# Strassen operands formed inside the evacuation of the first feed-forward block, an earlier input load, and a projection partly in single PSUM banks

## The chip, the cores and the metric

The kernel runs on one NeuronCore of a Trainium2 chip. Its five engines work from their own in-order queues and meet through semaphores: TensorE (PE in the profile, PEld for its weight loads), VectorE (DVE), ScalarE (ACT), GpSimd (POOL) and SyncE (SP), which issues every DMA here. The metric is the device time of one execution in microseconds, the median of several runs.

## The reference

One decoder layer runs on 512 prompt tokens and 8 single-token sequences, 520 columns in all, with a model width of 1024. Two recurrent branches come first. The part that matters here follows them:

```python
hm = rms_norm(r, norm_mlp_g)
r = r + jnp.square(jax.nn.relu(hm @ w_ff1)) @ w_ff2          # 1024 -> 4096 -> 1024
hp = rms_norm(r, norm_ple_g)
r = r + jax.nn.sigmoid(hp @ w_ple_gate) * (p_l @ w_ple_proj)  # per-layer inputs p_l, 256 wide
```

All of it is float32 work. A final RMS norm gives the outputs.

## The kernel before, in words

**Products in three passes.** Activations lie with channels on the 128 partitions and the 520 columns along the free side, cut in two halves of 260. Every operand is split into a rounded high part and a low rest (`H` and `L` for activations, `wh` and `wl` for weights), and each product is the sum of wh·H, wh·L and wl·H. A *unit* is one block of 128 output channels: 8 blocks of the contraction times 3 passes times 2 halves, so 48 matmuls of 128x128x260 into one PSUM tile `m`, which takes two banks. The pool of `m` has two buffers, so the third unit from now needs the tile of this one emptied. A second pool, `s`, has four single banks.

**The order.** There is no scheduler: `flow` is a list that the code writes by hand, and all engines get their instructions in that order. `run_unit(u)` first calls `prep_all()`, which prepares the weights of the item two places later in the list: ACT rounds `raw` to `wh` (L208), DVE subtracts to get `wl` (L213), and SP issues the next weight load. Then come the first 24 matmuls, the functions hooked to this unit in `at[u]`, the other 24 matmuls, and the unit's evacuation `evac`.

**The feed-forward part.** It computes 4096 hidden channels. The first quarter (1024) uses 8 plain units, `ff1`. Their evacuation `ev_ff1(i)` does relu times the norm's factor on DVE (tile `hid`, L942), the square on ACT (L943), and the split: the high part on ACT (L581), the low part on DVE (L582), into `fa` or `fb`. The other three quarters use a Strassen-Winograd scheme with seven products instead of eight: 12 *pairs* n = 0 to 11, each in four steps `(n, 0)` to `(n, 3)` of 24, 24, 24 and 12 matmuls into single banks X, Z and Y. Four sums of activations per contraction block kp = 0 to 3 are needed ahead of pair 0. `combine_a(kp)` scales two blocks of the residual stream (`hn`, L979, two instructions) and splits them into `comb`; `combine_b(kp)` forms four sums (`hs`, L994 to L997) and splits them into `comb` too. Before the change these are hooks in `at`, one to each ff1 unit from the second on, the last on the first unit of the following ff2 quarter.

**The second matrix.** `ff2` units turn a finished quarter of hidden channels back into the residual stream `xT` (L949). They are laid between the steps of the pairs: `(n,0)`, unit, `(n,1)`, `(n,2)`, unit, `(n,3)`. Two of the first quarter's ff2 units stand ahead of pair 0. That leaves six, so pairs 2 and 3 have no unit between `(n,0)` and `(n,1)`. A step's bank is read by ACT or DVE before a later product is added on top of it (L1037 is the copy of X that the product of `(n,1)` waits for).

**The projection.** `p_load` loads the per-layer inputs `pn` (SP, L1061) from a hook on the first ff2 unit of the last quarter, into the space S0 of a `comb` tile. `p_split` transposes them on PE (L1071) from a hook on the second. Two projection units follow. Each holds four groups of 12 matmuls, every group in an `m` tile, evacuated by one ACT copy per group (`pj`, L1084).

Of the kernel before, what the change touches and what calls it, by code (L numbers as in the profile page):

```python
# [45 lines left out]
def decoder_step_kernel(  # L46
# [179 lines left out]
    def mm(w, k, xh, xl, ps, first, last):  # L226
        wh, wl = w
        for i, (a, b) in enumerate(((wh, xh), (wh, xl), (wl, xh))):
            for z in range(2):
                PE.matmul(ps[:, z, :NH], lhsT=a[:, k, :], rhs=b[:, z * NH:(z + 1) * NH],  # L230
                          start=first and i == 0, stop=last and i == 2)

    psum_of = {}
# [1 line left out]
    def run_groups(u, lo, hi):  # L235

        due = []
        n = 0
        for gi, (slots, start, stop, evac) in enumerate(units[u].groups):
            for si, (k, xs) in enumerate(slots):  # L240
                if lo <= n < hi:
                    if si == 0 and start:
                        psum_of["cur"] = pm.tile([128, 2, 512], F32, tag="m", name="m")
                    ps = psum_of["cur"]
                    xh, xl = xs()
                    mm(w_of[u], k, xh, xl, ps, start and si == 0, stop and si == len(slots) - 1)
                    if si == len(slots) - 1 and evac is not None:
                        due.append((evac, ps))
                n += 1
        return due  # L250

    def run_unit(u):
        prep_all()
        if u in extra:
            prep_all()
        due = run_groups(u, 0, 4)
        for f in at.pop(u, []):
            f()
        for e, ps in due:
            e(ps[:, :, :NH])  # L260
        for e, ps in run_groups(u, 4, 8):
            e(ps[:, :, :NH])
        w_of.pop(u)

    def unit(w, c, H, L, evac):
# [670 lines left out]
    def ev_ff1(i):  # L936
        def ev(ps):
            if i == 0:
                mx["hid"] = pair("X2", "hid")
                hid_slots(0)  # L940
            t = mx["hid"][:, i % 2]
            V.scalar_tensor_tensor(h2(t), in0=ps, scalar=0.0, in1=h2(mx["rstd"]), op0=ALU.max, op1=ALU.mult)  # L942
            S.activation(t, t, AF.Square)  # L943
            split(hid[0][0][i], hid[0][1][i], t)
        return ev

    def ev_ff2(q, j):
# [21 lines left out]
    z0, z1 = slice(0, NH), slice(NH, N)  # L969

    def combine_a(kp):
        def go():
            r4 = lambda t: big.tile([128, 4, NH], F32R, tag=t, name="comb")
            if kp == 0:
                comb["A22"] = r4("S8"), r4("S9")
            n = comb["n"] = pair("S7", "hn")
            for h in range(2):
                j = kp + 4 * h
                V.scalar_tensor_tensor(n[:, h], in0=xT[:, j], scalar=cv[:, V_MLP + j:V_MLP + j + 1], in1=mx["rstd"],  # L979
                                       op0=ALU.mult, op1=ALU.mult)  # L980
            t = r4(f"S{10 + kp}")
            comb["A1", kp] = t[:, 0:2], t[:, 2:4]
            comb["S", kp] = r4(f"S{14 + kp}" if kp < 2 else f"S{kp - 2}"), r4(("S2", "S4", "S5", "S6")[kp])
            split(*comb["A1", kp], n[:, :, z0])
            H, L = comb["A22"]
            split(H[:, kp], L[:, kp], n[:, 1, z1])
        return go

    def combine_b(kp):
        def go():  # L990
            n = comb["n"]
            a11, a12, a21, a22 = n[:, 0, z0], n[:, 1, z0], n[:, 0, z1], n[:, 1, z1]
            t = big.tile([128, 4, NH], F32, tag="X0", name="hs")
            V.tensor_tensor(t[:, 0], a21, a22, op=ALU.subtract)  # L994
            V.tensor_tensor(t[:, 2], a11, a21, op=ALU.subtract)
            V.tensor_tensor(t[:, 1], t[:, 0], a11, op=ALU.subtract)
            V.tensor_tensor(t[:, 3], t[:, 1], a12, op=ALU.add)  # L997
            split(*comb["S", kp], t)
        return go
# [19 lines left out]
    def finish(q, slot, t):  # L1019
        S.activation(t, t, AF.Square)  # L1020
        split(hid[q][0][slot], hid[q][1][slot], t)

    def run_pair(n, i):

        q = 1 + n // 4
        slot = 2 * (n % 4)
        t1, t2 = mx["hid"][:, 0], mx["hid"][:, 1]
        prep_all()
        if i == 0:
            if slot == 0:  # L1030
                hid_slots(q)
# [3 lines left out]
        if i == 0:  # L1035
            product(n, 0, 0, "A11", X, True)
            S.activation(r1, X, AF.Copy)  # L1037
            product(n, 0, 1, "S1", Z, True)
            S.activation(r5, Z, AF.Copy)
        elif i == 1:  # L1040
            product(n, 1, 0, "S2", X, False)
            S.activation(r2, X, AF.Copy)
            Y = bank()[:, 0:NH]
            product(n, 1, 1, "A12", Y, True)
            V.tensor_tensor(t1[:, z0], r1, Y, op=ALU.add)
        elif i == 2:
            product(n, 2, 0, "S3", X, False)
            V.tensor_tensor(t2[:, z1], r5, X, op=ALU.subtract)
            product(n, 2, 1, "S4", Z, False)
            V.tensor_tensor(t2[:, z0], Z, r2, op=ALU.subtract)  # L1050
            S.activation(t2, t2, AF.Relu)
            finish(q, slot + 1, t2)
        else:
            S.activation(t1[:, z0], t1[:, z0], AF.Relu)
            product(n, 3, 0, "A22", X, False)
            S.activation(t1[:, z1], X, AF.Relu)
            finish(q, slot, t1)

    def p_load():
        mx["pn"] = big.tile([128, 4, 256], F32, tag="S0", name="pn")  # L1060
        dma(mx["pn"], p_prompt[0, 0].rearrange("(c p) d -> p c d", p=128))  # L1061
        dma(vd, p_sample[0, :, 0])

# [15 lines left out]
    def ev_proj(j):  # L1079
        def ev(ps):  # L1080
            if j == 0:
                for a in range(4):
                    mx["pj", a] = pair(f"S{8 + a}", "pj")
            S.activation(h2(mx["pj", j // 2][:, j % 2]), ps, AF.Copy, scale=0.5)  # L1084
# [9 lines left out]
        pair_src[n] = w1[:, :, 1024 + n * 256:1280 + n * 256]  # L1094
    flow = list(range(len(units)))
    ff2 = ff2_quarter(0)
    flow += ff2[:2]
    for kp in range(4):
        at[u_ff + 1 + 2 * kp].append(combine_a(kp))
        at[u_ff + 2 + 2 * kp].append(combine_b(kp))  # L1100
    ff2 = ff2[2:]
    for q in range(1, 4):
        per = (2, 2, 1, 1) if q == 1 else (2, 2, 2, 2)
        for n, m in zip(range(4 * q - 4, 4 * q), per):
            x, y = ff2[:m - 1], ff2[m - 1:m]
            ff2 = ff2[m:]
            flow += [(n, 0), *x, (n, 1), (n, 2), *y, (n, 3)]
        ff2 = ff2_quarter(q)
    u_proj = len(units)
# [8 lines left out]
                dma(rv[:, k], wpj[:, k, i * 512:(i + 1) * 512].rearrange("p (o n) -> p o n", n=128))  # L1118
        units.append(Unit(ld, groups))
    flow += [ff2[0], ff2[1], u_proj, u_proj + 1, *ff2[2:]]  # L1120
    at[ff2[0]].append(p_load)
    at[ff2[1]].append(p_split)


# [122 lines left out]
    plan_loads()  # L1247

    def run_ple():
        mx["gt"] = pair("S7", "gt").rearrange("p a n -> p (a n)")  # L1250
        mx["y"] = big.tile([128, 4, D], F32, tag="B1", name="y")
        mx["yd"] = big.tile([8, D], F32, tag="S6", name="yd")
        steps = defaultdict(list)
        for a, when in enumerate(((5, 7, 8, 10), (13, 14))):
            for jp, i in enumerate(when):
# [298 lines left out]
```

## Time and profile before

| | |
|---|---|
| median of three timed runs | 1118.9 us (1118.26 to 1120.29) |
| profiled execution, its own time | 1120.74 us |
| its span, first to last instruction | 1118.8 us |
| mean granted TensorE clock | 0.994 |
| PE busy | 1095.2 us (98%) |
| DVE busy | 652.6 us (58%) |
| ACT busy | 478.4 us (43%) |
| DMA moved | 123.01 MB, 110 GB/s mean |

Times in the views are microseconds from the first instruction, unless marked ns. A timeline row gives start, duration, engine, line, operation, output<-inputs, shapes, the number of merged instructions, and in brackets the idle time of that engine before it with what ended it. Busy PE time is an overlapped sum, so what a wait costs is read from the starts of PE's instructions. The waits view lists the total, the number and the longest of each kind of wait. The window view gives the busy time and number of instructions of each engine in a stretch, then the granted PE clock and the DMA's share and rate.

### The profile page before, as it was taken

Reading aid. Unit: us, or ns where it says so; the run is one execution under the profiler, and the core shown is the slowest. Engines: PE = TensorE matmul, PEld = TensorE weight load, DVE = VectorE, ACT = ScalarE, POOL = GpSimd, SP = SyncE. Lnnn points to the kernel's source line nnn. Section 1 sums busy time; section 2 is a strip of 40 time slices with the busy share of each in tenths; the row PEclk is TensorE's granted clock in tenths of the full one; section 3 lists DMA queues with packets and bytes.
Section 4 is the critical chain, followed back from the end, with each engine's and each line's share of the span. In section 5 each row is a group of like instructions: output and inputs, shape, how many; then the busy total and the mean of one; then the engine's idle time right before and its main releaser. Section 6 shows DMA issues by size and latency. Waiting matters only on the chain.

```text
span 1118.8 us, 23371 instructions
## 1 busy us (share of the span) xinstructions
PE 1095.2 (98%) x10289; PEld 1075.1 (96%) x10289; DVE 652.6 (58%) x989; ACT 478.4 (43%) x765; POOL 24.4 (2%) x19
## 2 busy tenths in 40 slices
PE   8999999999999999999999999799899999999997
PEld 8999999999999999999999999799899999999997
DVE  6576767859656754442342555665756666653665
ACT  6322534343344425422222244434545445544465
POOL 1000000000011011000000000000000000000001
PEclk9999999999999999999999999989999999999999
DMA  6535252533445365433333232223232432343401
GB/s 218 152 96 170 82 170 73 157 105 115 136 138 156 114 173 154 118 95 95 95 88 101 77 95 76 76 76 95 76 114 77 114 112 76 103 133 87 112 20 77
DMA packets 218740, 123.01 MB, mean 110 GB/s; under 512 B 3960, under 2 KB 217216, under 8 KB 218512
## 3 DMA queue, kind: packets, MB, share of 16 engines
q1 hardware_dynamic: 218640, 121.54, 37.7%
q8 instruction: 80, 1.31, 0.5%
q14 instruction: 20, 0.16, 0.0%
HBM read 109.89 MB, written 11.63 MB: 109 GB/s over the span
## 4 chain that ended last, share of the span: by engine, by line
PE 93%; DVE 3%; ACT 3%; DMA 1%; issue 1%; SPq 0%; DVEq 0%; ACTq 0%
PE m L230 67%; PE s L1014 10%; PE m L1279 2%; PE s L1279 2%; PE s L363 1%; PE s L482 1%; ACT wh L208 1%; DVE wl L213 1%; PE s L765 1%; PE s L519 1%; PE s L543 1%; PE s L722 1%; DVE comb L582 1%; DMA pn<-in_p_prompt_dram 0%; PE s L545 0%
## 5 line engine op out<-in xcount | busy, mean ns | idle before, releaser
L213 DVE TENSOR_TENSOR wl<-raw,wh 128x1024 fp32r<-128x1024 f32 (+1 forms) x141 | 172.8, 1227 | 128.5 <-ACT wh L208 128.0
L230 PE MATMUL m<-hH,wh 128*128 128x260 f32 x1120 | 230.9, 287 | 0.0
L230 PE MATMUL m<-hH,wl 128*128 128x260 f32 x1120 | 226.0, 283 | 0.0
L230 PE MATMUL m<-hL,wh 128*128 128x260 f32 x1120 | 225.2, 283 | 0.0
L208 ACT ACTIVATE wh<-raw 128x1024 fp32r<-128x1024 f32 (+1 forms) x141 | 147.3, 1046 | 84.8 <-PE m L230 78.9
L230 PEld LDWEIGHTS m<-hH,wh 128*128 128x128 f32 x1120 | 172.3, 188 | 3.4 <-issue 1.7
L230 PEld LDWEIGHTS m<-hH,wl 128*128 128x128 f32 x1120 | 172.5, 188 | 0.0
L230 PEld LDWEIGHTS m<-hL,wh 128*128 128x128 f32 x1120 | 172.5, 188 | 0.0
L1014 PE MATMUL s<-comb,wh 128*128 128x260 f32 x672 | 122.4, 283 | 3.1 <-ACT cst L1037 3.1
L1014 PEld LDWEIGHTS s<-comb,wh 128*128 128x128 f32 x672 | 103.8, 188 | 3.5 <-ACT cst L1037 3.5
L1014 PE MATMUL s<-comb,wl 128*128 128x260 f32 x336 | 95.1, 283 | 0.0
L230 PE MATMUL m<-fa,wh 128*128 128x260 f32 x384 | 69.3, 291 | 3.7 <-DVE hid L942 2.0
L1014 PEld LDWEIGHTS s<-comb,wl 128*128 128x128 f32 x336 | 63.2, 188 | 0.0
L230 PEld LDWEIGHTS m<-fa,wh 128*128 128x128 f32 x384 | 57.1, 196 | 4.1 <-issue 2.2
L230 PE MATMUL m<-fa,wl 128*128 128x260 f32 x256 | 52.6, 288 | 0.0
L230 PE MATMUL m<-fl,wh 128*128 128x260 f32 x256 | 52.2, 286 | 0.0
L230 PE MATMUL m<-fh,wh 128*128 128x260 f32 x256 | 52.1, 285 | 0.0
L230 PE MATMUL m<-fh,wl 128*128 128x260 f32 x256 | 51.9, 284 | 0.0
L949 DVE TENSOR_TENSOR xT<-xT,m 128x520 f32<-128x520 f32 x32 | 22.3, 696 | 40.7 <-PE m L230 40.7
L164 ACT ACTIVATE wh<-cst 128x512 fp32r<-128x512 f32 x36 | 22.8, 633 | 43.5 <-DVE cst L170 29.1
L230 PEld LDWEIGHTS m<-fa,wl 128*128 128x128 f32 x256 | 40.6, 194 | 0.0
L230 PEld LDWEIGHTS m<-fh,wl 128*128 128x128 f32 x256 | 40.1, 192 | 0.0
(356 smaller groups left out, 2000.5 us busy)
## 6 DMA issues: line engine op xcount, KB each, us to landing
raw<-in_w_in_dram SPq DMA_DIRECT2D x72, 512.0 KB, 3.9
raw<-in_w_ff_dram SPq DMA_DIRECT2D x40, 512.0 KB, 4.1
rawp<-in_w_ff_dram SPq DMA_DIRECT2D x24, 512.0 KB, 3.7
vbc<-vdd SPq DMA_DIRECT2D x16, 512.0 KB, 4.2
Sd<-in_state_hgrn_dram SPq DMA_DIRECT2D x8, 512.0 KB, 8.0
out_dram<-Sd SPq DMA_DIRECT2D x8, 512.0 KB, 5.4
rSd<-in_state_ret_dram SPq DMA_DIRECT2D x8, 512.0 KB, 5.9
out_dram<-rSd SPq DMA_DIRECT2D x8, 512.0 KB, 3.5
```

What stands on the lines that cost most here:

```text
L164: S.activation(wh[:, 4 * h:4 * h + 4], x, AF.Copy)
L208: S.activation(wh[:, k], r[:, k], AF.Copy)
L213: e1.tensor_sub(wl[:, k], r[:, k], wh[:, k])
L230: PE.matmul(ps[:, z, :NH], lhsT=a[:, k, :], rhs=b[:, z * NH:(z + 1) * NH], start=first and i == 0, stop=last and i == 2)
L363: PE.matmul(b[32 * j:32 * j + 32, 32 * hc:32 * hc + 32], lhsT=kx[:, h, o:o + 32], rhs=qx[:, h, o:o + 32], start=True, stop=True)
L482: PE.matmul(b[32 * i:32 * i + 32, :], lhsT=q[g], rhs=Sd[g][:, 4 * z:4 * z + 4, :], start=True, stop=True)
L519: PE.matmul(b[:, c * 128:(c + 1) * 128], lhsT=kn[:, h, c, :], rhs=vn[:, h, c, :], start=True, stop=True)
L543: PE.matmul(o, lhsT=vn[:, h, c, :], rhs=A[:, h * 4 + c, :], start=True, stop=c == 0)
L582: V.tensor_sub(L, x, H)
L949: V.tensor_tensor(h2(xT[:, j]), h2(xT[:, j]), ps, op=ALU.add)
L1014: PE.matmul(out, lhsT=w[:, 4 * half + k, :], rhs=x, start=start and k == 0 and m == 0, stop=k == 3 and m == 2, skip_group_check=not start)
L1279: PE.matmul(ps, lhsT=w[:, k, :], rhs=x, start=k == 0 and n == 0, stop=k == 7 and n == 2)
```

## The change

1. **Sums inside the evacuation.** `combine_a` and `combine_b` no longer are hooks. `ev_ff1(i)` calls one of them itself: a for even i, b for odd i. It puts the DVE arithmetic between the square and the split, appends ACT's high parts of `comb` behind the split, and leaves only DVE's subtractions as a hook of the next unit.
2. **Order of the first quarter's pairs.** One ff2 unit instead of two stands ahead of pair 0. Pairs 0, 1 and 2 have two units each. Pair 3 has the one between `(3,0)` and `(3,1)` and none between `(3,2)` and `(3,3)`. In `(3,2)` the weight preparation moves from the step's start to behind the first product's DVE subtraction (`prep_last`).
3. **Load of the per-layer inputs.** `p_load` is hooked one unit earlier, to the last ff2 unit of the third quarter, and its tile lies in S7 (the old `hn`). `gt` moves from S7 to S6, and `yd` from S6 to S7.
4. **Projection banks.** In each projection unit groups 0 and 1 keep an `m` tile. Groups 2 and 3 take two single banks each and are evacuated by two ACT copies of 260 columns.

The diff, cut to its core:

```diff
@@ run_groups @@
-                        psum_of["cur"] = pm.tile([128, 2, 512], F32, tag="m", name="m")
-                    ps = psum_of["cur"]
+                        if gi < 2:
+                            t = pm.tile([128, 2, 512], F32, tag="m", name="m")
+                            psum_of["cur"] = t[:, :, :NH], [t[:, z, :NH] for z in range(2)]
+                        else:
+                            psum_of["cur"] = None, [bank()[:, :NH] for z in range(2)]
+                    both, ps = psum_of["cur"]
...
@@ ev_ff1 @@
             S.activation(t, t, AF.Square)
+            cuts = combine_b(i // 2) if i % 2 else combine_a(i // 2)
             split(hid[0][0][i], hid[0][1][i], t)
+            for c in cuts:
+                S.activation(c[0], c[2], AF.Copy)
+            at[u_ff + i + 1].append(lambda: [V.tensor_sub(x, y, h) for h, x, y in cuts])
...
@@ run_pair @@
-        prep_all()
+        if (n, i) not in prep_last:
+            prep_all()
...
             product(n, 2, 0, "S3", X, False)
             V.tensor_tensor(t2[:, z1], r5, X, op=ALU.subtract)
+            if (n, i) in prep_last:
+                prep_all()
             product(n, 2, 1, "S4", Z, False)
...
@@ p_load @@
-        mx["pn"] = big.tile([128, 4, 256], F32, tag="S0", name="pn")
+        mx["pn"] = big.tile([128, 4, 256], F32, tag="S7", name="pn")
...
@@ ev_proj @@
+            out = mx["pj", j // 2][:, j % 2]
+            if isinstance(ps, list):
+                for z in range(2):
+                    S.activation(out[:, z * NH:(z + 1) * NH], ps[z], AF.Copy, scale=0.5)
+            else:
+                S.activation(h2(out), ps, AF.Copy, scale=0.5)
...
@@ flow @@
-    flow += ff2[:2]
-    for kp in range(4):
-        at[u_ff + 1 + 2 * kp].append(combine_a(kp))
-        at[u_ff + 2 + 2 * kp].append(combine_b(kp))
-    ff2 = ff2[2:]
+    flow += ff2[:1]
+    ff2 = ff2[1:]
     for q in range(1, 4):
-        per = (2, 2, 1, 1) if q == 1 else (2, 2, 2, 2)
+        per = (2, 2, 2, 1) if q == 1 else (2, 2, 2, 2)
...
-            x, y = ff2[:m - 1], ff2[m - 1:m]
+            x, y = ff2[:1], ff2[1:m]
             ff2 = ff2[m:]
+            if not y:
+                prep_last.add((n, 2))
             flow += [(n, 0), *x, (n, 1), (n, 2), *y, (n, 3)]
...
-    at[ff2[0]].append(p_load)
+    at[ff2[0] - 1].append(p_load)
```

**Where instructions move.** The first place is DVE's queue in the ff1 units, from one `hid` to the next. Before:

```order
L942 SCALAR_TENSOR_TENSOR hid<-m,x_7811 128x520
L582 TENSOR_TENSOR fb<-hid,fa 128x520
L213 TENSOR_TENSOR wl<-raw,wh 128x1024
L994 TENSOR_TENSOR hs<-hn 128x260
L995 TENSOR_TENSOR hs<-hn 128x260
L996 TENSOR_TENSOR hs<-hs,hn 128x260
L997 TENSOR_TENSOR hs<-hs,hn 128x260
L582 TENSOR_TENSOR comb<-hs,comb 128x1040
L942 SCALAR_TENSOR_TENSOR hid<-m,x_7811 128x520
```

And in the changed kernel, on the same stretch (fb is the low part of the split, wl that of the weights two units ahead):

```order
L947 SCALAR_TENSOR_TENSOR hid<-m,x_7811 128x520
L999 TENSOR_TENSOR hs<-hn 128x260
L1000 TENSOR_TENSOR hs<-hn 128x260
L1001 TENSOR_TENSOR hs<-hs,hn 128x260
L1002 TENSOR_TENSOR hs<-hs,hn 128x260
L587 TENSOR_TENSOR fb<-hid,fa 128x520
L214 TENSOR_TENSOR wl<-raw,wh 128x1024
L953 TENSOR_TENSOR comb<-hs,comb 128x1040
L947 SCALAR_TENSOR_TENSOR hid<-m,x_7811 128x520
```

The four sums stand right behind `hid` instead of behind `wl`. The subtraction stays last. ACT's rounding of `comb` moves in the same way, from behind `wh` to ahead of it.

The second place is ACT's queue from the last step of pair 2 on, in the changed kernel: steps `(3,1)`, `(3,2)`, `(3,3)` and the beginning of what follows. L1048 is the copy in `(3,1)`. L1059 to L586 are the relu, square and high part of the pair's second block. L1062 and L1064 are the two relus in `(3,3)`, of which L1064 empties bank X:

```order
L165 ACTIVATE wh<-cst 128x512
L1048 ACTIVATE cst<-s 128x260
L165 ACTIVATE wh<-rawp 128x512
L165 ACTIVATE wh<-cst 128x512
L1059 ACTIVATE hid<-hid 128x520
L1024 ACTIVATE hid<-hid 128x520
L586 ACTIVATE fh<-hid 128x520
L209 ACTIVATE wh<-raw 128x1024
L1062 ACTIVATE hid<-hid 128x260
L1064 ACTIVATE hid<-s 128x260
```

Before, the same pair's ACT rows, from its copy in `(3,1)`, were these:

```order
L1042 ACTIVATE cst<-s 128x260
L164 ACTIVATE wh<-cst 128x512
L1051 ACTIVATE hid<-hid 128x520
L1020 ACTIVATE hid<-hid 128x520
L581 ACTIVATE fh<-hid 128x520
L164 ACTIVATE wh<-rawp 128x512
L164 ACTIVATE wh<-cst 128x512
L208 ACTIVATE wh<-raw 128x1024
L1054 ACTIVATE hid<-hid 128x260
L1056 ACTIVATE hid<-s 128x260
```

The two half roundings (rawp and cst) move from behind the split to ahead of the relu. The unit that stood ahead of `(3,3)` is gone, so all of this falls into fewer matmuls.

The third place is SP's queue of loads, before:

```order
L965 DMA raw<-in_w_ff_dram 128x8x128 x3
L1118 DMA raw<-in_w_ple_proj_dram 128x4x128 x4
L965 DMA raw<-in_w_ff_dram 128x8x128 x2
L1061 DMA pn<-in_p_prompt_dram 128x4x256
L1062 DMA vd<-in_p_sample_dram 8x256
L224 DMA raw<-in_w_ple_gate_dram 128x8x128
```

And now:

```order
L974 DMA raw<-in_w_ff_dram 128x8x128 x3
L1130 DMA raw<-in_w_ple_proj_dram 128x4x128 x4
L1069 DMA pn<-in_p_prompt_dram 128x4x256
L1070 DMA vd<-in_p_sample_dram 8x256
L974 DMA raw<-in_w_ff_dram 128x8x128 x2
L225 DMA raw<-in_w_ple_gate_dram 128x8x128
```

The inputs `pn` and `vd` pass two weight loads.

More of the change, by code (lines that the diff above doesn't have):

```diff
@@ L118, in decoder_step_kernel @@
     extra = set()
+    prep_last = set()
     raw_of, w_of = {}, {}
@@ L229, in mm @@
             for z in range(2):
-                PE.matmul(ps[:, z, :NH], lhsT=a[:, k, :], rhs=b[:, z * NH:(z + 1) * NH],
+                PE.matmul(ps[z], lhsT=a[:, k, :], rhs=b[:, z * NH:(z + 1) * NH],
                           start=first and i == 0, stop=last and i == 2)
@@ L247, in run_groups @@
                     if si == len(slots) - 1 and evac is not None:
-                        due.append((evac, ps))
+                        due.append((evac, both if both is not None else ps))
                 n += 1
@@ L259, in run_unit @@
         for e, ps in due:
-            e(ps[:, :, :NH])
+            e(ps)
         for e, ps in run_groups(u, 4, 8):
-            e(ps[:, :, :NH])
+            e(ps)
         w_of.pop(u)
@@ L971, in combine_a @@
     def combine_a(kp):
[L972 to L986, printed above, removed]
@@ L987, in combine_a @@
-        return go
-    def combine_b(kp):
[L990 to L999, printed above, removed]
+        r4 = lambda t: big.tile([128, 4, NH], F32R, tag=t, name="comb")
@@ new lines, in combine_a @@
+        if kp == 0:
+            comb["A22"] = r4("S8"), r4("S9")
+        n = comb["n"] = pair("S7", "hn")
+        for h in range(2):
+            j = kp + 4 * h
+            V.scalar_tensor_tensor(n[:, h], in0=xT[:, j], scalar=cv[:, V_MLP + j:V_MLP + j + 1], in1=mx["rstd"],
+                                   op0=ALU.mult, op1=ALU.mult)
+        t = r4(f"S{10 + kp}")
+        comb["A1", kp] = t[:, 0:2], t[:, 2:4]
+        comb["S", kp] = r4(f"S{14 + kp}" if kp < 2 else f"S{kp - 2}"), r4(("S2", "S4", "S5", "S6")[kp])
@@ new lines, in combine_a @@
+        return (*comb["A1", kp], n[:, :, z0]), (*(x[:, kp] for x in comb["A22"]), n[:, 1, z1])
+    def combine_b(kp):
+        n = comb["n"]
+        a11, a12, a21, a22 = n[:, 0, z0], n[:, 1, z0], n[:, 0, z1], n[:, 1, z1]
+        t = big.tile([128, 4, NH], F32, tag="X0", name="hs")
+        V.tensor_tensor(t[:, 0], a21, a22, op=ALU.subtract)
+        V.tensor_tensor(t[:, 2], a11, a21, op=ALU.subtract)
+        V.tensor_tensor(t[:, 1], t[:, 0], a11, op=ALU.subtract)
+        V.tensor_tensor(t[:, 3], t[:, 1], a12, op=ALU.add)
+        return (*comb["S", kp], t),
@@ L1083, in ev @@
                     mx["pj", a] = pair(f"S{8 + a}", "pj")
-            S.activation(h2(mx["pj", j // 2][:, j % 2]), ps, AF.Copy, scale=0.5)
+            out = mx["pj", j // 2][:, j % 2]
[4 more added lines that the diff above has]
+                S.activation(h2(out), ps, AF.Copy, scale=0.5)
         return ev
@@ L1249, in run_ple @@
     def run_ple():
-        mx["gt"] = pair("S7", "gt").rearrange("p a n -> p (a n)")
+        mx["gt"] = pair("S6", "gt").rearrange("p a n -> p (a n)")
         mx["y"] = big.tile([128, 4, D], F32, tag="B1", name="y")
-        mx["yd"] = big.tile([8, D], F32, tag="S6", name="yd")
+        mx["yd"] = big.tile([8, D], F32, tag="S7", name="yd")
         steps = defaultdict(list)
```

## The prediction

> **What bounds the kernel now.** I read the chain of waits first, then PE's waits, then PE's own starts where the waits are.
>
> ```profile
> PE 93%; DVE 3%; ACT 3%; DMA 1%; issue 1%; SPq 0%; DVEq 0%; ACTq 0%
> 468.38 206.89 PE m L230 x1728
> ```
>
> The chain is PE nearly throughout. Its undisturbed stretch gives the pitch: 206.89 / 1728 = 0.1197 us a matmul, so 5.75 us a unit of 48 and 1.44 us a product of 12. The change keeps every matmul, so it can win only what PE waits.
>
> ```profile
> PE m L230 <- DVE hid L942: 5.8, 4, 2.0
> PE m L1371 <- DMA xs<-in_x_sample_dram: 3.4, 1, 3.4
> PE s L1014 <- ACT cst L1037: 3.1, 2, 1.6
> PE m L230 <- ACT fa L581: 1.7, 1, 1.7
> PE s L1071 <- DMA pn<-in_p_prompt_dram: 1.3, 1, 1.3
> PE m L1192 <- DVE sqs L1164: 0.9, 1, 0.9
> PE m L230 <- ACT pj L1084: 0.9, 2, 0.7
> ```
>
> All but the second and sixth row lie in places that the change touches: the ff1 units (hid, fa), pairs 2 and 3 (cst), the load pn and the projection (pj). What they cost with their aftermath is read from PE's weight-load starts:
>
> ```profile
> 679.23 0.30 PEld L230 LDWEIGHTS m<-hmH,wh 128*128 128x128 f32 x2
> ...
> 726.23 0.81 PEld L230 LDWEIGHTS m<-fa,wh 128*128 128x128 f32 x4 [2.22 <-issue]
> ...
> 734.74 0.30 PEld L230 LDWEIGHTS m<-fa,wh 128*128 128x128 f32 x2 [1.91 <-ACT fa L581]
> ...
> 743.19 0.31 PEld L1014 LDWEIGHTS s<-comb,wh 128*128 128x128 f32 x2
> ```
>
> From the second ff1 unit (679.23) to pair 0 (743.19) are 63.96 us for 9 units, which need 9 x 5.75 = 51.7. So 12.2 us are lost here, more than the waits' 7.5. The rest is the clock, halved after some waits:
>
> ```profile
> 727.00:730.00 3.00, 3.00 (x16) 3.00 (x16) 2.27 (x3) 1.40 (x2) 0.00 (x0) 0.53 0.00 0
> ```
>
> PE gets 16 matmuls done in 3.00 us where 25 fit, at a granted 0.53.
>
> Why PE waits there is DVE's and ACT's chain from one evacuation to the next:
>
> ```profile
> 694.90 0.69 DVE L942 SCALAR_TENSOR_TENSOR hid<-m,x 128x520 f32<-128x520 f32 x1
> 696.96 0.70 DVE L582 TENSOR_TENSOR fa<-hid,fa 128x520 fp32r<-128x520 f32 x1 [1.37 <-ACT fa L581]
> 697.91 1.23 DVE L213 TENSOR_TENSOR wl<-raw,wh 128x1024 fp32r<-128x1024 f32 x1 [0.25 <-ACT wh L208]
> 699.05 1.43 DVE L979 SCALAR_TENSOR_TENSOR hn<-xT,cv,x 128x520 f32<-128x520 f32 x2
> 701.18 1.04 DVE L582 TENSOR_TENSOR comb<-hn,comb 128x520 fp32r<-128x520 f32 x2 [0.70 <-ACT comb L581]
> 702.14 0.69 DVE L942 SCALAR_TENSOR_TENSOR hid<-m,x 128x520 f32<-128x520 f32 x1
> 704.21 0.70 DVE L582 TENSOR_TENSOR fa<-hid,fa 128x520 fp32r<-128x520 f32 x1 [1.38 <-ACT fa L581]
> 705.16 1.23 DVE L213 TENSOR_TENSOR wl<-raw,wh 128x1024 fp32r<-128x1024 f32 x1 [0.25 <-ACT wh L208]
> 706.30 0.42 DVE L994 TENSOR_TENSOR hs<-hn 128x260 f32<-128x260 f32 x1
> ...
> 709.01 1.24 DVE L582 TENSOR_TENSOR comb<-hs,comb 128x1040 fp32r<-128x1040 f32 x1 [1.14 <-ACT comb L581]
> 710.17 0.69 DVE L942 SCALAR_TENSOR_TENSOR hid<-m,x 128x520 f32<-128x520 f32 x1
> ```
>
> The period is 7.24 us with hn and 8.03 with hs, mean 7.64, against PE's 5.75. DVE works only some 5 of it. It idles 1.4 behind ACT's square and split, and 0.7 or 1.1 behind ACT's rounding of comb.
>
> **A. Sums inside the evacuation.** The same instructions run, in another order, and none is added. ACT's links come from here:
>
> ```profile
> 700.51 0.95 ACT L581 ACTIVATE comb<-hn 128x520 fp32r<-128x520 f32 x2 [2.63 <-DVE hn L979]
> 702.87 0.64 ACT L943 ACTIVATE hid<-hid 128x520 f32<-128x520 f32 x1 [1.40 <-DVE hid L942]
> 703.53 0.64 ACT L581 ACTIVATE fa<-hid 128x520 fp32r<-128x520 f32 x1
> 704.08 1.05 ACT L208 ACTIVATE wh<-raw 128x1024 fp32r<-128x1024 f32 x1
> 707.90 1.07 ACT L581 ACTIVATE comb<-hs 128x1040 fp32r<-128x1040 f32 x1 [2.77 <-DVE hs L997]
> ```
>
> With hid starting at 0, the square starts at 0.73, the split's copy at 1.39, and ACT is free at 1.94. Meanwhile hn starts on DVE at 0.61 and is ready for ACT 1.46 later (699.05 to 700.51), at 2.07. ACT then rounds comb (0.95, the next starts 0.1 before its end), so wh starts at 2.92 and wl 1.08 later at 4.00. The comb subtraction follows 1.14 after that (697.91 to 699.05) and the next hid 0.96 later: a period of 6.1. With hs: ready at 0.61 + 1.60 = 2.21, wh at 3.18, wl at 4.26, comb at 5.40, hid 1.16 later: 6.56. The split's own subtraction (ready at 2.06) fits ahead of wl. So the mean falls to 6.33. The last evacuation comes 5.8 after the one before it, as the weights prepared there are two halves (0.6 each) of pair 0.
>
> The first evacuation starts two periods before 694.90, at 679.6. Then the seventh comes at 679.6 + 3 x 12.66 = 717.6 and frees its tile by 718.4. PE wants that tile at 679.23 + 7 x 5.75 = 719.5, so none of the tile waits is left, with 1 us to spare. The eighth starts at 723.4, and its high part ends 2.04 later at 725.4. PE wants it in the last eighth of the first ff2 unit, at 719.5 + 5.0 = 724.5: a wait of 0.9, and about 0.5 more for the low part (0.70 of DVE less the two matmuls on the high part). Pair 0 starts at about 726.7. Its second product needs the last comb sums, whose subtraction ends 5.40 + 1.24 after the last hid, at 730.0, and PE wants them at 729.3: 0.7 more. Left are 2.1 of the 12.2, so A gains **10.1**. In general, with mean period P over the seven, the gain is about 53.8 - 7P: 0.3 at the old 7.64 (the loss of cover by one ff2 unit eats the rest), 10 here. Below nothing comes only from P above 7.7.
>
> **B. Pairs 2 and 3.** Pair 2 gets the order of pairs 0 and 1, which show no wait. Pair 3 keeps a unit behind `(3,0)`. The 3.1 of the two cst waits go. In return `(3,2)`, `(3,3)`, `(4,0)` now follow each other. The second product of `(4,0)` goes to the bank X of pair 3, the fourth bank back, and so waits until L1064 has emptied it. ACT's way there:
>
> ```profile
> 987.93 0.64 ACT L1051 ACTIVATE hid<-hid 128x520 f32<-128x520 f32 x1 [2.81 <-DVE hid L1050]
> ...
> 994.64 0.39 ACT L1056 ACTIVATE hid<-s 128x260 f32<-128x260 f32 x1 [0.31 <-PE s L1014]
> ```
>
> From the start of `(3,1)`, the first product of `(3,2)` is done at 3 x 1.44 = 4.3, plus 0.2 to DVE. DVE does one subtraction (0.36), one sum (0.6) and two weight subtractions, the second behind ACT's second half rounding (to 6.9), and only then the subtraction that the relu waits for. Relu 0.46 later (7.3), square 8.0, high part 8.7, wh 9.2, the two relus 10.2 and 10.5, X empty at 10.9. PE wants it at 6 x 1.44 = 8.7: a wait of **2.2**. Behind it stand PE's whole queue, first the next unit. The lower bound is 1.2, if DVE's weight work does not hold up its subtraction (ready 0.9 earlier); the upper 3.6, with a half clock after it. I take 2.2, since DVE runs in order. B gains 3.1 - 2.2 = **0.9**.
>
> **C. Load and projection.**
>
> ```profile
> 995.31 3.67 SPq L965 DMA_DIRECT2D raw<-in_w_ff_dram  x2
> 999.03 0.96 SPq L1061 DMA_DIRECT2D pn<-in_p_prompt_dram  x1
> 1006.00:1009.70 3.70, 3.70 (x19) 3.70 (x19) 1.28 (x3) 0.59 (x2) 0.00 (x0) 0.54 0.44 131
> ```
>
> pn stood behind two weight loads that wait for their buffers. Ahead of them it issues by 995.31 at the latest, 3.7 earlier, which covers the 1.3 wait twice. Its new space, the last hn, was read for the last time around pair 0's start (743.19). The two weight loads shift by the 1.4 that pn and vd take to issue. Their weights are prepared two units (11 us) later, so this costs nothing; without that cover, 1.4. With the wait goes the half-rate window behind it: 19 matmuls in 3.70 where 31 fit, 12 x 0.1197 = 1.4. Gain **2.7**; 1.3 if the sparse transposes alone still halve the clock. The projection's groups 2 and 3 no longer wait for pj: gain **0.9**. Two copies of 260 (0.39 as at 994.64) replace one of 520 (0.64 as at 702.87) in four groups. PE's next product (1.44) hides the extra 0.14 of each; without that cover it would be 0.6 in all.
>
> **Sum.** 10.1 + 0.9 + 2.7 + 0.9 = 14.6. The new wait of 2.2 is as long as the one at 726.23, after which the clock fell, so it may cost 1.4 more; half of that, 0.7, is charged: 13.9. On the profiled execution's own 1120.7 that gives 1106.8. The timed median is 1.8 lower than it, so the forecast is **1105**.
>
> [...]
>
> **Rivals.**
> 1. *The waits that are left are shorter.* A keeps 1.0 instead of 2.1, B 1.2 instead of 2.2, and the clock never falls: 1.1 + 1.0 + 0.7 = 2.8 better, 1102. For it: the 12.2 us lost exceed their waits by 4.5, only about three halved windows at 1.4, so not every wait brings one. Against it: ACT's links behind the relu are in strict order.
> 2. *Half the shortening.* If ACT's comb rounding starts later than DVE's sums allow, P stays near 7.0: A gains 53.8 - 49 = 4.8, less 1.4 for a halved clock, 3.4. The sum is 3.4 + 0.9 + 3.6 - 0.7 = 7.2: 1111.7. Against it: each link was measured with the same neighbour.
> 3. *The change does not do what it says*: the hid waits are paced by the raw loads or the wp buffers rather than the chain, the period stays, and C's gain meets B's new wait and a halved clock: 0.3 + 3.6 + 0.9 - 1.4 - 1.4 = 2.0, 1116.9; 1118 with a second such window. Against it: no row above names a DMA.
> 4. *Slower.* The evacuation becomes fully serial: DVE's sums stand ahead of the split, and if the square and the split's copy start only behind them, the hs link sum is 0.73 + 1.60 + 0.67 + 0.67 + 1.07 + 1.08 + 1.14 + 1.16 = 8.1, plus 0.6 for the split's subtraction ahead of wl, 8.7; with hn about 8.3. P = 8.5 loses 53.8 - 59.5 = -5.7 and two clock windows (2.8) against 4.5 from B and C: 4.0 slower, 1122.9. It decides from P = 8.3. Against it: the square needs only hid, which precedes the sums.
>
> **How the numbers follow.** Forecast 0.60, rival 1 0.16, rival 2 0.15, rival 3 0.05, rival 4 0.04. The forecast's own spread is about 2.5 either way: 1 us of slack in A, the clock, and the 1.8 between profile and median. The range 1100.5 to 1111 leaves out rivals 3 and 4, over half of rival 2 and a little of rival 1. A difference under 0.2% (2.2 us) cannot be told from none; rival 3 lies on that bound and is split: faster 0.93, same 0.03, slower 0.04.
>
> **What would show it.** Right: no PE wait for hid in the ff1 units, periods of 6.1 and 6.6; a wait of about 1 us for fa and 0.7 for comb; no cst wait in pairs 2 and 3, but one of about 2 us at the second product of pair 4; no wait for pn and none for pj. Wrong: hid waits that remain, or a granted clock near 0.5 in stretches where I count none.

## The result, and the profile after

The median went from 1119.6 us (1118.26 to 1120.54) to 1102.98 us (1102.3 to 1103.59): ratio 0.9852, 95% interval 0.9835 to 0.9869. A second comparison on another chip gave 1117.41 and 1103.59, ratio 0.9869 (0.9854 to 0.9885). So the gain is 14 to 17 us. The profiled execution after has a span of 1100.5 us and its own time is 1102.48; the mean granted clock is 0.998.

The chain of waits of the changed kernel is again PE nearly throughout, and the undisturbed weight blocks are unchanged to the last digit:

```profile
PE 93%; DVE 4%; ACT 2%; issue 1%; DMA 0%; SPq 0%; DVEq 0%
467.15 206.89 PE m L231 x1728
```

So nothing was saved in the work itself. The gain is in PE's waits (total, number, longest):

```profile
PE m L1383 <- DMA xs<-in_x_sample_dram: 3.3, 1, 3.3
PE m L1204 <- DVE sqs L1176: 0.9, 1, 0.9
PE m L231 <- DVE wl L214: 0.5, 1, 0.5
PE s L1018 <- DVE comb L953: 0.5, 1, 0.5
PE m L231 <- ACT fa L586: 0.5, 1, 0.5
...
PE m L231 <- DVE fb L587: 0.2, 1, 0.2
```

The rows for `hid`, `cst`, `pn` and `pj` are gone, and `fa` has fallen from 1.7. New are one wait for `wl` and one for `comb`. The first two rows were there before and lie elsewhere. Why `hid` is no longer waited for shows in DVE's timeline of the changed kernel:

```profile
691.05 0.69 DVE L947 SCALAR_TENSOR_TENSOR hid<-m,x 128x520 f32<-128x520 f32 x1
691.65 1.42 DVE L988 SCALAR_TENSOR_TENSOR hn<-xT,cv,x 128x520 f32<-128x520 f32 x2
693.12 0.70 DVE L587 TENSOR_TENSOR fa<-hid,fa 128x520 fp32r<-128x520 f32 x1
695.04 1.23 DVE L214 TENSOR_TENSOR wl<-raw,wh 128x1024 fp32r<-128x1024 f32 x1 [1.22 <-ACT wh L209]
696.18 1.03 DVE L953 TENSOR_TENSOR comb<-hn,comb 128x520 fp32r<-128x520 f32 x2
697.13 0.69 DVE L947 SCALAR_TENSOR_TENSOR hid<-m,x 128x520 f32<-128x520 f32 x1
...
701.39 1.23 DVE L214 TENSOR_TENSOR wl<-raw,wh 128x1024 fp32r<-128x1024 f32 x1 [1.47 <-ACT wh L209]
702.53 1.23 DVE L953 TENSOR_TENSOR comb<-hs,comb 128x1040 fp32r<-128x1040 f32 x1
703.68 0.69 DVE L947 SCALAR_TENSOR_TENSOR hid<-m,x 128x520 f32<-128x520 f32 x1
```

From `hid` to `hid` are 6.08 us with hn and 6.55 with hs, where the kernel before took 7.24 and 8.03. DVE now idles in one place, behind ACT's `wh`, instead of three (1.37, 0.25 and 0.70 in the period with hn).

The waits that are left show in PE's weight loads of the changed kernel, around pair 0 and behind pair 3:

```profile
724.14 0.30 PEld L231 LDWEIGHTS m<-fa,wh 128*128 128x128 f32 x2 [0.67 <-ACT fa L586]
724.90 0.30 PEld L231 LDWEIGHTS m<-fb,wh 128*128 128x128 f32 x2 [0.46 <-DVE fb L587]
...
728.75 0.19 PEld L1018 LDWEIGHTS s<-comb,wh 128*128 128x128 f32 x1 [0.68 <-DVE comb L953]
...
808.25 0.30 PEld L1018 LDWEIGHTS s<-comb,wh 128*128 128x128 f32 x2
...
810.01 0.30 PEld L231 LDWEIGHTS m<-fh,wh 128*128 128x128 f32 x2 [0.26 <-ACT wh L209]
...
811.27 0.30 PEld L231 LDWEIGHTS m<-fh,wl 128*128 128x128 f32 x2 [0.72 <-DVE wl L214]
```

Each bracket is the idle time alone. Measured by how late PE's matmuls start against its pitch of 0.12, these waits cost 0.63, 0.41 and 0.63 around pair 0, and 0.21 and 0.68 behind pair 3. The second product of `(4,0)` loads its first weights at 808.25 without a wait.

In the 405 us between 660 and 1065 PE did 3203 matmuls before and does 3346 now. At 0.1197 each, that leaves 21.6 us in which it did none before, and 4.5 now. A window view of the stretch with the pairs of the first quarter, of the kernel before and then of the changed one (columns: length, then busy time and instructions of PE, PEld, DVE, ACT and POOL, granted clock, DMA share, GB/s), says the same:

```profile
670.00:820.00 150.00, 139.19 (x1118) 137.54 (x1117) 95.03 (x143) 70.75 (x115) 0.00 (x0) 0.98 0.28 82
```

```profile
670.00:820.00 150.00, 148.24 (x1223) 147.09 (x1223) 102.06 (x155) 78.10 (x128) 0.00 (x0) 1.00 0.32 92
990.60:994.00 3.40, 3.40 (x29) 3.40 (x29) 1.60 (x5) 0.59 (x2) 0.00 (x0) 1.00 0.55 154
```

In equal time some 100 more matmuls were done, and the clock is whole. The last row is the stretch behind the transposes of pn, where the profile before had 19 matmuls in 3.70 us at 0.54.

### The profile page after: what moved, and what is told of

Its sections match the earlier page's. It is cut to its first block, busy times and chain, and to the rows that moved or that the text cites. A ratio compares the mean times of both kernels' runs of the same rounds, so it can differ in the third digit from the quotient of the medians.

```text
span 1100.5 us, 23371 instructions
## 1 busy us (share of the span) xinstructions
PE 1087.8 (99%) x10289; PEld 1068.4 (97%) x10289; DVE 652.6 (59%) x989; ACT 478.9 (44%) x769; POOL 23.9 (2%) x19
## 4 chain that ended last, share of the span: by engine, by line
PE 93%; DVE 4%; ACT 2%; issue 1%; DMA 0%; SPq 0%; DVEq 0%
PE m L231 67%; PE s L1018 10%; PE m L1291 2%; PE s L1291 2%; PE s L368 1%; DVE wl L214 1%; PE s L487 1%; DVE comb L953 1%; ACT wh L209 1%; PE s L548 1%; PE s L770 1%; PE s L524 1%; PE s L727 1%; PE s L231 1%; PE s L550 0%
## 5 line engine op out<-in xcount | busy, mean ns | idle before, releaser
L209 ACT ACTIVATE wh<-raw 128x1024 fp32r<-128x1024 f32 (+1 forms) x141 | 147.4, 1047 | 84.5 <-PE m L231 80.5
L231 PE MATMUL m<-fa,wh 128*128 128x260 f32 x384 | 67.0, 283 | 0.5 <-ACT fa L586 0.5
L231 PEld LDWEIGHTS m<-fa,wh 128*128 128x128 f32 x384 | 54.7, 188 | 0.7 <-ACT fa L586 0.7
L231 PEld LDWEIGHTS m<-fh,wh 128*128 128x128 f32 x256 | 39.3, 188 | 0.3 <-ACT wh L209 0.3
```

Source lines behind the costliest of these rows:

```text
L209: S.activation(wh[:, k], r[:, k], AF.Copy)
L231: PE.matmul(ps[z], lhsT=a[:, k, :], rhs=b[:, z * NH:(z + 1) * NH], start=first and i == 0, stop=last and i == 2)
```

## The experiments

### One edit at a time

Four kernels, each the kernel before with one edit of the change, timed together (before: 1118.09 us). **Edit 1 alone**, the sums inside the evacuation:

```diff
@@ ev_ff1 @@
             S.activation(t, t, AF.Square)
+            cuts = combine_b(i // 2) if i % 2 else combine_a(i // 2)
             split(hid[0][0][i], hid[0][1][i], t)
+            for c in cuts:
+                S.activation(c[0], c[2], AF.Copy)
+            at[u_ff + i + 1].append(lambda: [V.tensor_sub(x, y, h) for h, x, y in cuts])
...
```

> The kernel before with edit 1 alone: the sums formed inside the evacuation, the old order of the pairs, the old load, the old banks. Theory (the period of the evacuations falls from 7.64 us to 6.33 in the mean, so PE's waits for hid go): PE waits for hid 0, about 0.7 for fa and 0.5 for fb, no wait for comb since two ff2 units cover it, the two cst waits of pairs 2 and 3 stay; the stretch from the second ff1 unit to pair 0 shrinks from 64.0 us to about 53, and the time falls by 10 to 11 us. Rival (the order of the pairs brings the gain there, since one ff2 unit fewer stands in front): the waits for hid stay above 4 us and the time falls by less than 3.

Measured: 1108.82 us, ratio 0.991 (0.9896 to 0.9923), so 9.3 us faster. Its waits on PE:

```profile
PE s L1013 <- ACT cst L1036: 3.1, 2, 1.6
PE s L1070 <- DMA pn<-in_p_prompt_dram: 1.3, 1, 1.3
...
PE m L230 <- ACT pj L1083: 0.9, 2, 0.7
PE m L230 <- ACT fa L581: 0.8, 1, 0.8
```

The 5.8 of `hid` are gone, `fa` falls from 1.7 to 0.8, and the other rows stay. The stretch from the second ff1 unit to pair 0 takes 53.5 us in this profile, as expected, though the timed gain is a little under the 10 to 11 expected. This edit by itself gives 9.3 of the 14 to 17 us.

**Edit 2 alone**, the order of the pairs:

```diff
@@ flow @@
-    flow += ff2[:2]
+    flow += ff2[:1]
...
-        per = (2, 2, 1, 1) if q == 1 else (2, 2, 2, 2)
+        per = (2, 2, 2, 1) if q == 1 else (2, 2, 2, 2)
...
+            if not y:
+                prep_last.add((n, 2))
...
```

> The kernel before with edit 2 alone: one ff2 unit ahead of pair 0, the new spread of the units over pairs 0 to 3, and the late weight preparation in pair 3; the sums stay hooks. Theory: the waits for hid stay near 5.8, the cst waits of 3.1 go and about 1.1 appears at the unit behind pair 3; but pair 0 now comes 5.8 us sooner than the last comb sums and waits for them about 1.3 us, with perhaps a halved clock behind it: the time falls by 0 to 2 us. Rival (the pairs' order brings the gain in the ff1 stretch): the time falls by 8 or more.

Measured: 1117.67 us, ratio 0.9993 (0.9984 to 1.0002): no difference that can be told. Its waits on PE say where the 3.1 us of `cst` went:

```profile
PE m L231 <- DVE hid L943: 5.8, 4, 2.1
...
PE m L231 <- ACT fa L582: 2.2, 1, 2.2
...
PE m L231 <- DVE wl L214: 0.5, 1, 0.5
PE s L1015 <- DVE comb L583: 0.4, 1, 0.4
```

`fa` rose from 1.7 to 2.2, and waits for `comb` and `wl` are new. The ff2 unit taken from ahead of pair 0 had covered the late last evacuation. Without edit 1 the cover is missed. By PE's starts these waits take back 2.0 us of the 3.4 that the `cst` waits had cost. The other 1.4 can't be told from none: the interval of the time reaches to 1.8 us faster.

**Edit 3 alone**, the load moved ahead:

```diff
-        mx["pn"] = big.tile([128, 4, 256], F32, tag="S0", name="pn")
+        mx["pn"] = big.tile([128, 4, 256], F32, tag="S7", name="pn")
...
-    at[ff2[0]].append(p_load)
+    at[ff2[0] - 1].append(p_load)
...
```

> The kernel before with edit 3 alone: the per-layer inputs are loaded one unit earlier and lie in S7. Theory: the wait of 1.3 us for pn goes, and with it the halved clock behind it (1.4): 2.7 to 3.1 us faster. Rival (the sparse transposes alone halve the clock): 1.3 to 1.5 faster, and a granted clock near 0.5 behind the transposes stays.

Measured: 1116.36 us, ratio 0.9983 (0.9974 to 0.9992), 1.7 us faster. The wait for pn is gone and the clock stays whole behind it: two weight loads take 0.30 to 0.31 us there, where the kernel before took 0.55. That is about 1 us less than expected, but the interval runs from 0.9 to 2.9 us and does not rule the expectation out.

**Edit 4 alone**, two of four projection groups in the small banks:

```diff
...
+                        if gi < 2:
+                            t = pm.tile([128, 2, 512], F32, tag="m", name="m")
+                            psum_of["cur"] = t[:, :, :NH], [t[:, z, :NH] for z in range(2)]
+                        else:
+                            psum_of["cur"] = None, [bank()[:, :NH] for z in range(2)]
...
```

> The kernel before with edit 4 alone: groups 2 and 3 of each projection unit in two single banks. Theory: the two pj waits (0.9 us by the waits view, 1.4 in PE's starts) go and nothing else moves: 0.9 to 1.4 us faster, hardly to be told from none by time, but the waits view shows it. Rival (the extra ACT copies push the weight roundings back): a wait for wl or wh appears in the units behind the projection, and the time stays or rises.

Measured: 1116.13 us, ratio 0.9979 (0.997 to 0.9988), 2.0 us faster (1.3 to 3.4 by the interval), more than expected. The waits for `pj` are gone (counted by PE's starts, they cost 0.83 + 0.37 = 1.2 us before). In its profile the load of pn is still waited for, in PE's weight loads:

```profile
1002.65 0.42 PEld L1075 LDWEIGHTS s<-cid,pn 128*128 128x128 f32 x4 [1.26 <-DMA pn<-in_p_prompt_dram]
```

Yet no matmul behind it is slow: two weight loads take 0.30 to 0.31 us there too. Nor was one in the profile of edit 2 alone, after a longer wait of 1.56, while behind the 1.47 in the kernel before and the 1.49 in edit 1 alone the clock was halved (0.50 granted from 1006.30 to 1009.72 us in the one, and 16 matmuls in 3.04 us at 0.50 in the other). So much the same wait brings a halved stretch in one execution and none in another. The last experiment shows what decides it.

The four gains add up to 13.4 us, against 16.6 and 13.8 for all of them together. With intervals 2 to 4 us wide, these times agree with edits that add, and can't show more.

### The waits that are left

Four kernels timed together (before: 1117.41). One is the changed kernel again, with nothing edited:

> The changed kernel once more, on the same chip as the two kernels made from it: 1102 to 1104 us, and in the trace the same waits: about 0.5 each for fa and fb and 0.5 for comb ahead of and in pair 0, and 0.5 for wl in the unit behind pair 3.

Measured: 1103.59 us (1103.46 to 1103.83), with the same waits. Yet its profiled span is 1.1 us longer than the one above, of the same kernel. The window view of the first stage, of this execution and then of the one above, shows where that comes from:

```profile
8.80:12.80 4.00, 4.00 (x22) 3.98 (x22) 2.20 (x6) 2.05 (x7) 2.81 (x3) 1.00 1.09 349
8.80:12.80 4.00, 3.60 (x32) 3.37 (x32) 3.37 (x9) 3.31 (x10) 2.70 (x3) 1.00 1.10 352
```

Here PE starts a matmul every 0.21 us until about 12.5 us; above, they come 0.11 apart from about 9 us, but for one wait. (The view's clock column does not tell them apart this early.) All twelve profiles of this document are of one or the other kind: six, the kernel before among them, have 21 or 22 matmuls in this window, and six have 30 to 36 and stand 0.9 to 1.4 us ahead from then on. Times are therefore best compared between executions of one kind. The timed spans of the changed kernel show both: 1100.5, and 1101.6 to 1101.8.

**Rounding behind the weights.** By the prediction's working, ACT's rounding of `comb` (0.95 to 1.07 us) stands ahead of `wh`, and all of DVE's later links hang on `wh`. If that is the link that counts, moving only this back behind `wh`, while the sums stay early, must shorten the period further. The rival is that the late rounding then holds up the `comb` subtraction, as it did before the change.

```diff
@@ ev_ff1, against the changed kernel @@
-            for c in cuts:
-                S.activation(c[0], c[2], AF.Copy)
+            at[u_ff + i + 1].append(lambda: [S.activation(h, y, AF.Copy) for h, x, y in cuts])
             at[u_ff + i + 1].append(lambda: [V.tensor_sub(x, y, h) for h, x, y in cuts])
```

> The changed kernel with ACT's rounding of comb put back behind the weights' rounding wh (as a hook of the next unit), the DVE sums staying right behind hid. Theory (the period is the chain hid, sums, comb rounding, wh, wl, comb subtraction): comb's rounding now runs beside DVE's wl, the period falls from 6.1 and 6.6 us to about 5.1 and 5.3, under PE's 5.75, so hid follows PE: the waits for fa, fb and comb ahead of and in pair 0 go (about 2.0 us in PE's starts) and the period is set by PE, 5.75: 1.5 to 2.2 us faster than the changed kernel. Rival (it is the place of the rounding ahead of wh that won the time): the period returns towards 7.6, hid waits come back and the time rises by 8 or more.

Measured: 1100.61 us (1100.45 to 1101.73), ratio to before 0.9847 (0.983 to 0.9863), 3.0 us faster than the changed kernel beside it. But all four of that one's executions have the longer span. Between executions of one kind the gain is about 1.9 us (spans of 1098.5 to 1098.7 against 1100.5, and 1099.7 or 1099.8 against 1101.6 to 1101.8), within the expected 1.5 to 2.2. DVE's timeline:

```profile
695.74 0.70 DVE L947 SCALAR_TENSOR_TENSOR hid<-m,x 128x520 f32<-128x520 f32 x1 [0.56 <-PE m L231]
...
697.84 0.69 DVE L587 TENSOR_TENSOR fa<-hid,fa 128x520 fp32r<-128x520 f32 x1
698.77 1.23 DVE L214 TENSOR_TENSOR wl<-raw,wh 128x1024 fp32r<-128x1024 f32 x1 [0.24 <-ACT wh L209]
699.91 1.23 DVE L952 TENSOR_TENSOR comb<-hs,comb 128x1040 fp32r<-128x1040 f32 x1
701.51 0.70 DVE L947 SCALAR_TENSOR_TENSOR hid<-m,x 128x520 f32<-128x520 f32 x1 [0.36 <-PE m L231]
```

`hid` now waits for PE's matmuls. Its period is PE's own 5.77, and the waits for `fa`, `fb` and `comb` at pair 0 are gone. Both rivals fall, the period's return towards 7.6 and this one: `comb` follows `wl` without idle time, since DVE's 1.23 on `wl` covers ACT's rounding of 0.93 to 1.06.

**The preparation in pair 3.** `prep_last` puts the weight work of `(3,2)` behind its first product's subtraction. Is that needed? The changed kernel without it:

```diff
@@ flow, against the changed kernel @@
-            if not y:
-                prep_last.add((n, 2))
```

> The changed kernel without the late weight preparation in pair 3: it stands at the start of (3,2) again. A look at the trace, since less than 1 us is at stake. Theory (ACT's chain relu, square, high part, wh sets the unit behind pair 3): the relu starts about 0.8 us earlier, so the wait for wl there falls from 1.1 to about 0.4 us, and the product of (3,3) may wait 0.1 to 0.2 for DVE. Rival (the late preparation is what keeps PE fed): a wait of over 1 us for DVE appears at (3,3) or in pair 4.

Measured in one execution: 1102.81 us, span 1100.9, beside 1101.6 for the changed kernel's profile of the same kind. Of 0.9 us only this is left, at the start of `(3,3)`, in PE's weight loads:

```profile
806.80 0.30 PEld L1018 LDWEIGHTS s<-comb,wh 128*128 128x128 f32 x2 [0.15 <-DVE hid L1054]
```

PE starts 0.1 us late here, and no longer waits for `wl`. In this one execution, then, the late preparation costs more than it protects.

**Both.** The rounding moved back, and the weights of the unit behind pair 3 prepared one step earlier, in `(3,2)`, ahead of its relu:

```diff
@@ run_pair, against the kernel with the rounding moved @@
-        if (n, i) not in prep_last:
+        if (n, i) not in prep_last and (n, i - 1) not in prep_last:
             prep_all()
...
             V.tensor_tensor(t2[:, z0], Z, r2, op=ALU.subtract)
+            if (n, i) in prep_last:
+                prep_all()
             S.activation(t2, t2, AF.Relu)
```

> As the run before, and in pair 3 the weight preparation of the unit behind it stands in step (3,2), ahead of the relu on ACT, instead of in (3,3). Theory: the wait for wl at that unit (1.1 us in PE's starts) goes as well: about 3 us faster than the changed kernel, 1099.5 to 1100.5. Rival (the unit waits for DVE's other work): the wait stays.

Measured: 1099.9 us (1099.04 to 1100.57), ratio 0.9836 (0.9819 to 0.9852), 3.7 us faster than the changed kernel. It beats both kernels. Between executions of one kind (spans of 1097.3 and 1097.5, 1098.5 and 1098.7) it is 3.1 us faster than the changed kernel, as expected, and 1.1 to 1.2 faster than with the rounding alone. In ACT's timeline `wh` for the unit (L209) now stands ahead of the relu (L1060), which was the order that mattered:

```profile
805.05 1.04 ACT L209 ACTIVATE wh<-raw 128x1024 fp32r<-128x1024 f32 x1
806.24 0.64 ACT L1060 ACTIVATE hid<-hid 128x520 f32<-128x520 f32 x1
```

The window view of the same kernel has nothing left to win in this stretch:

```profile
670.00:820.00 150.00, 150.00 (x1248) 149.88 (x1247) 104.75 (x158) 78.16 (x129) 0.00 (x0) 1.00 0.33 94
```

### When the clock is halved

Half a halved window was charged in the prediction. To see what length of wait brings one, the changed kernel got waits of graded length: in step `(n, 1)` of pairs 1 to 11 ACT's copy of X, on which the product adds, is repeated 4 + n more times, and in a second kernel 16 - n more times. Nothing is left out; the copies only repeat.

```diff
@@ run_pair, against the changed kernel @@
+STALL = {n: 4 + n for n in range(1, 12)}
...
             product(n, 1, 0, "S2", X, False)
-            S.activation(r2, X, AF.Copy)
+            for _ in range(1 + STALL.get(n, 0)):
+                S.activation(r2, X, AF.Copy)
```

> The changed kernel with waits of graded length put in front of PE, to price a wait's aftermath: in step (n,1) of pairs 1 to 11 ACT copies bank X again and again to the same place, 4 + n times more than needed, and PE's next product onto X waits for the last copy. At about 0.3 us a copy PE waits 0.5 to 3.3 us, once per pair, some 21 us apart. Theory 1 (the clock halves when PE idled for more than about 1.9 us within one window of about 3.4 us of a free-running grid): no slow matmuls behind waits under 1.8, slow ones behind some of those of 2.0 to 3.0 and behind all of over 3.6, 15 or 16 matmuls at 0.215 us each time. Theory 2 (only an idle time of a full 3.4 us window halves the clock): no slow matmuls behind any wait up to 3.3.

> The same with the waits in reverse order: 16 - n copies more in pair n, so the longest comes first. Theory 1: the same lengths are followed by slow matmuls where the wait lies within one window and not where a window's border cuts it, so lengths near 2 us can come out otherwise than in the run before. Theory 2: none.

Measured: 1152.12 and 1152.76 us, one execution each. A repeated copy took 0.42 us (by so much the wait grows with each copy more), more than was assumed, so the waits run from 1.4 to 5.5 us instead of 0.5 to 3.3. Three of the first kernel's waits and what PE did behind them, in its weight loads (about 0.30 for two loads at the full clock, 0.50 to 0.55 at half):

```profile
827.57 0.50 PEld L1021 LDWEIGHTS s<-comb,wh 128*128 128x128 f32 x2 [2.61 <-ACT cst L1052]
...
853.62 0.30 PEld L1021 LDWEIGHTS s<-comb,wh 128*128 128x128 f32 x2 [3.03 <-ACT cst L1052]
...
854.75 0.55 PEld L1021 LDWEIGHTS s<-comb,wh 128*128 128x128 f32 x2
...
880.23 0.30 PEld L1021 LDWEIGHTS s<-comb,wh 128*128 128x128 f32 x2 [3.45 <-ACT cst L1052]
```

And one of the second kernel's, with the waits in falling order:

```profile
926.45 0.30 PEld L1021 LDWEIGHTS s<-comb,wh 128*128 128x128 f32 x2 [3.02 <-ACT cst L1052]
```

An idle of 2.61 halved the clock at once, 3.03 halved it 1.0 us after work had begun again, and 3.45 and the other 3.02 did not halve it. So in these runs length alone didn't decide. The granted clock shows what did: in the first kernel the half-clock stretches between 820 and 1030 us end at 830.68, 857.99, 909.19, 936.50, 963.80, 994.52 and 1021.83 us, whose distances are whole multiples of 3.413 (8, 15, 8, 8, 9 and 8 times). In the kernel before 0.50 was granted from 726.41 to 729.82, 736.65 to 740.06 and 1006.30 to 1009.72: each stretch is 3.41 us long, and they start 3 and 79 such steps apart. So in these traces the clock changed on the borders of a grid of that width. These are four windows of the grid: the one in which most of the 3.03 lies with the one behind it, and the two into which a border cuts the 3.45:

```profile
851.17:854.58 3.41, 0.96 (x8) 0.96 (x9) 0.55 (x2) 2.75 (x7) 0.00 (x0) 1.00 0.46 151
854.58:857.99 3.41, 3.41 (x18) 3.41 (x17) 0.66 (x2) 0.00 (x0) 0.00 (x0) 0.50 0.00 0
875.06:878.47 3.41, 1.93 (x17) 1.72 (x15) 1.60 (x2) 2.69 (x7) 0.00 (x0) 1.00 0.41 117
878.47:881.88 3.41, 1.65 (x13) 1.65 (x14) 0.69 (x1) 2.10 (x6) 0.00 (x0) 1.00 0.22 73
```

Take as PE's idle time in a window what its matmuls, at 0.119 us from start to start, leave of the 3.41. It is 2.57 in the first of these windows, and 1.67 and 1.88 in the last two, behind which the clock stayed whole. From the ff1 units to the projection, over all twelve profiles, each window that began at full clock and had at least 2.1 us idle was followed by half clock, and each with at most 1.98 by full clock. Of the two between, 1.99 halved it and 2.01 did not. The windows with the transposes of pn are left out of this count: there 1.86 and 1.89 were enough. Windows already at half clock were followed by full clock with at most 0.76 us idle (a matmul taken as 0.215), and by a second one at half with 1.05 or more. Counted in matmuls both limits lie at 11 to 13 in a window.

So of the expected theories the first held, with its limit near 2.0 us, and the second fell with the 2.61: about 2 of the 3.41 us were enough, so a window need not be idle throughout. The kernels of the change fit as well. In the kernel before, the waits around 726 and 735 us left 2.24 and 2.11 us idle in one window each, and each was followed by half clock. In the two profiles of the changed kernel no window from the ff1 units to the projection has more than 1.24. For pn, all of the 1.47 in the kernel before lies in the window from 1002.89 to 1006.30, while a border at 1002.83 cuts the 1.56 of edit 2 alone.

## Why the prediction was right, and where it was not

The forecast was 1105.0 and the measured median is 1102.98, inside the range. The sum was made for the profiled execution, though, and there it gave 1106.8 against 1102.48: 4.3 us too little gain.

**A held.** The predicted periods of 6.1 and 6.56 came out as 6.08 and 6.55. The `hid` waits went. Left were 0.63 (predicted 0.9), 0.41 (0.5) and 0.63 (0.7): 1.7 against 2.1. Edit 1 alone showed that this is its doing, and moving the rounding showed that the strict order of ACT's links is the reason: the prediction's link of 0.95 to 1.07 us ahead of `wh` is what kept the period above PE's. Two side readings were off. The rule 53.8 - 7P gives 9.5 at 6.33, not 10. And the 12.2 us held two halved windows, not about three: by PE's starts the waits alone had cost 8.6, where the waits view gave 7.5.

**B's step failed: "The second product of `(4,0)` goes to the bank X of pair 3, the fourth bank back, and so waits until L1064 has emptied it."** ACT's way was worked out rightly, as its timeline in the changed kernel shows:

```profile
807.03 0.64 ACT L1059 ACTIVATE hid<-hid 128x520 f32<-128x520 f32 x1 [1.10 <-DVE hid L1058]
...
808.92 1.04 ACT L209 ACTIVATE wh<-raw 128x1024 fp32r<-128x1024 f32 x1
...
810.17 0.37 ACT L1064 ACTIVATE hid<-s 128x260 f32<-128x260 f32 x1
```

`(3,1)` starts at 799.72, so L1064 starts 10.45 us behind it; 10.5 was worked out. But the product had already been under way since 808.25, while X was still to be read. It writes another bank: in the built program it is the bank of Y of pair 3, which DVE had emptied in `(3,1)`. The banks were counted off in the order of their allocation, and this pool doesn't hand them out in that order. What the late ACT chain did delay is the next item in its queue, the weights of the ff2 unit: `wh` at 808.92, and `wl` on DVE behind it. That wait is 0.21 + 0.68 = 0.9 instead of 2.2, and the clock stayed whole. B thus gained 2.6 us in PE's starts (3.4 lost before, 0.9 after), where 0.9 was forecast, and the 0.7 charged for the clock wasn't due. The prediction named `wh` at 9.2 in this chain and didn't ask who waits for it.

**C held in its mechanism.** SP's queue in the changed kernel:

```profile
979.24 0.46 SPq L1069 DMA_DIRECT2D pn<-in_p_prompt_dram  x1
...
981.40 3.67 SPq L974 DMA_DIRECT2D raw<-in_w_ff_dram  x2
```

pn issues ahead of the two weight loads, there is no wait for it, and the shifted loads cost nothing. The two copies per group are hidden, as worked out. `pj` was mis-sized: 0.9 was taken from the waits view, but PE's starts were 1.2 late. The term of 1.4 for the halved clock was right for this one execution, but not for each: of the four profiles that kept the wait two had it. Edit 3 alone gained 1.7, with an interval that leaves both open.

**Profile and median.** The forecast took 1.8 off because the profiled execution before lay that much above its median of three runs (1.1 above the median of four given here). The one after lies 0.5 below its own. From the ff1 units to the projection three halved stretches were in the profile before and none in the one after, and the profile before is of the kind with 0.21 us a matmul until about 12.8 us. That these make up the 1.8 fits, but is argued, not shown. If they do, the aftermath of the stalls was counted as gain and then taken off once more with the excess. Without the 1.8 the forecast would have been 1106.8, 3.8 us off instead of 2.0. So it is in part luck that it came this near: a step taken for another reason made up for part of the gain that B's term had missed.

The 4.3 us of the profiled execution are thus B's 1.7 and the clock's 0.7, 0.4 of A, 0.3 of `pj`, and 1.2 that has nothing to do with the change: PE stands 1.2 us earlier by 98 us, in a stage that the change doesn't touch, since the execution before has its matmuls at 0.21 us until about 12.8 us and the one after only until about 8. Together 4.3.

Of the rivals, the first (1102) has the nearest time. Its whole clock came, and its 1.2 for what is left in B is nearer to the 0.9 that came than the forecast's 2.2. A kept 1.7, between its 1.0 and the forecast's 2.1. Half the shortening, no shortening and a serial evacuation are out by the periods above.

## What to carry to other kernels

Where PE waits for an evacuation, lay out one period of the other engines link by link and ask which instruction in an in-order queue stands ahead of something that others wait for: moving early sums ahead of the split gave 9.3 us, and moving one rounding back behind the weight rounding about 2 more. When a chain is late, follow every product of it to its consumer, and take the bank that a tile gets from the built program instead of counting. Whether a slow stretch follows a short wait depended here on where the wait fell, and that changed from one execution to the next (of the four profiles with the wait for pn, of 1.26 to 1.56 us, two had one): count it with its chance, and not again in the step from the profile to the median. And where executions fall into two kinds, compare within one.

## What was not expected of the hardware

The clock was not halved by a wait's length alone: in the kernel with rising waits one of 2.61 us brought a slow stretch and one of 3.45 didn't, depending on how much of it fell into one window of a 3.41 us grid, with the limit near 2 us. Copies that repeated on the same source and target followed each other in 0.42 us on ACT (waits of 2.61, 3.03 and 3.45 us in neighbouring pairs, one copy apart). And the spans of otherwise equal executions differ by a step of about 1.2 us (1100.5 and 1101.6 to 1101.8 for the changed kernel): in six of the twelve profiles PE's matmuls come 0.21 us apart until about 13 us, and in the other six they come at 0.11 from about 9 us on.
